# Gated norm of a hybrid gMLP/Mamba-2 layer: sums of squares by ones in column tiles, factors through memory, two gate blocks kept on chip

## The chip, the cores and the metric

The kernel runs on one core of a Trainium2 chip. The time is the device time of one execution in microseconds (us); of the kernel before there are three runs, 1413.58, 1413.98 and 1417.91 us, with the median 1413.98 us. One more execution was profiled. PE is TensorE (matrix products, and transposes as products with an identity), PEld its weight loads, DVE VectorE, ACT ScalarE, POOL GpSimd, and SP the engine that only issues loads. ACT issues all stores besides its own work.

## What is computed

One layer of a model with sequence length 1024 and width 1024, in float32. Of the reference these parts matter:

```python
y_a = spatial_gating(gelu(gm_u), gelu(gm_v), ...) * silu(gm_z)
y_b = ssd_scan(xh, dt, a, bm, cm) + xh * d_skip[:, None]          # 8 groups of 4 heads of 64 channels, chunks of 128
yz = (y_b.reshape(b, s, 2048) * silu(ssm_z)).reshape(b, s, 8, 256)
y_b = rms_norm(yz, ssm_norm_w.reshape(8, -1)).reshape(b, s, 2048)  # the gated norm: over 256 channels of a group
merged = sigmoid(g_a) * (y_a @ w_proj_a) + sigmoid(g_b) * (y_b @ w_proj_b)
x = x + gate[:, None, :] * (merged @ w_out)
return rms_norm(x, final_norm_w)
```

The gated norm needs for each group and each of the 1024 positions one factor, (sum of 256 squares / 256 + 1e-6) to the power -0.5.

## The kernel before

Channels lie on the 128 partitions and positions along the free dimension. Up to about 955 us the kernel makes the modulation, h and the large product with `w_in`. Then, to about 1150 us, it runs the SSD stage, to about 1319 us the second projection (units of p1, p2, p5, p3, p6, p7, p4), and last the product with `w_out`.

**The SSD stage** is a loop over 32 steps (L1434 on). A step is one group g of the eight and one s of 0 to 3, a quarter of the positions (256); the groups are taken in pairs, so the steps run 0_0, 1_0, 0_1, 1_1, 0_2 and so on, then 2_0, 3_0 on. A step takes some 6.3 us. In step n the program writes, in this order: `decay_rows` of step n+3 (ACT: two exponentials `ea`; POOL: an `AFFINE_SELECT` that masks `dcy`), `front` of step n (PE: `yi`, `sp`; DVE: `y1` and the state `st`; POOL: decay of the state), a few products of the first projection as filler (`proj_a`, tile `pma`, handed out by `draw`), `back` of step n (PE: `yn`; DVE: `ym`; POOL: `y` and then `yz`, the gated output), `prep_products` of step n+2 (PE: `pc`, `px`; DVE: `dcy` times `pc`), `decay_exps` of step n+3 (ACT: eight exponentials on `dcy`), `prep_b` of step n+2 (ACT: a copy `bn` of a part of `pc`, after which the PSUM bank of `pc` is given to the next tile that asks for one) and `fetch` of step n+6 (SP: loads of `dcy` and `sl`). From the last pair of products with `w_in` on, so in all that is told here, every engine runs its instructions in the order in which the program writes them.

**The factors before.** Two steps of a group fill one tile `yz` of 512 positions (q = 0 or 1). When it is full, `post` puts off the rest by slots of a task list (`later(k, f)`: f is written k slots on; a step has three slots): the stores of `yz` to `yb_d` after 3, the squares (ACT, and a sum of two halves on POOL) after 9, `post2` after 17. `post2` makes the column sums with `yz` as weights and a column of ones as moving operand: four products, each in two passes since the data are float32, with one PSUM column of 128 positions each (`pq`, 128x4). A slot later `post2b` brings them to `ssq` on DVE; with q = 1 (for groups 6 and 7 with each q) POOL takes the power -0.5 (`roots`), and 8 slots on `post3` transposes the 128x8 (or 128x4) of `ssq` on PE (`pr`; in the second projection the four of groups 6 and 7 go to a bank of `yp`), copies the rows on DVE and stores them to `rs_d`. The second projection loads `rs_d` as `rb` and `yb_d` as `yn`, multiplies them on DVE and splits the result on ACT (`p1bh`, with `p1a` for its weights).

**The first projection** `proj_a` (L1350) makes eight blocks dd of 128 rows in two halves: loads a gate `tha` on SP when the block begins, sums `pma`, multiplies (L1374) and stores to `mt_d` on ACT; the second projection loads that as `ma` (L1577) and adds it.

**Queues.** Stores stand in ACT's order among its arithmetic, loads in SP's order; an instruction that waits holds up those behind it on its engine. Each DMA also waits for an earlier one, some eight issues back, whose completion counter it takes over.

Of the kernel before, what the change touches and what calls it, by code (L numbers as in the profile page):

```python
# [35 lines left out]
def hybrid_kernel(  # L36
# [34 lines left out]
    rs_d = [dt_([1, S], f"rs_d{g}") for g in range(NG)]  # L71
    v_d = dt_([NG, P, NCH * P], "v_d")
# [887 lines left out]
    class Group:  # L960
# [158 lines left out]
        def post(self, q):  # L1119
# [8 lines left out]
            if g < NG - 2 or q == 0:  # L1128
                later(3, leave)
                later(9, self.squares, yz, [yz[:, j] for j in range(2)])  # L1130
                later(17, self.post2, q, yz[:, 0])
            else:
                wait = 1 if g < NG - 1 else 3
                later(wait, leave)
                sq = [turn(r, f"sq{g}", F32) for r in ((y1_r, ym_r) if g < NG - 1 else (war_r[0], war_r[0]))]
                later(wait, self.squares, yz, sq, pin)
                later(9, self.post2, q, sq[0])
# [6 lines left out]
        def post2(self, q, sq):  # L1144
            g = self.g
            pq = bank(f"pq{g}_{q}")
            for i in range(4):
                mm(pq[:, i : i + 1], sq[:, i * P : (i + 1) * P], ones[:, 0:1])
            later(1, self.post2b, q, pq)

        def post2b(self, q, pq):
            g = self.g
            V.tensor_scalar(ssq[:, g * NCH + q * 4 : g * NCH + q * 4 + 4], pq[:, 0:4], 1.0 / 256, EPS,
                            op0=ALU.mult, op1=ALU.add)
            release(f"pq{g}_{q}")
            if g >= NG - 2:
                self.roots(4 * q, 4)
            elif q == 1:
                self.roots(0, NCH)
                later(8, self.post3, 0, NCH)  # L1160

        def roots(self, c0, n):
            cs = slice(self.g * NCH + c0, self.g * NCH + c0 + n)
            G.tensor_tensor(ssq[:, cs], ssq[:, cs], nhalf[:, 0:n], op=ALU.pow)

        def post3(self, c0, n, at_once=False):

            g = self.g
            pr = rows_bank[0](f"pr{g}")
            tp(pr[0:n, 0:P], ssq[:, g * NCH + c0 : g * NCH + c0 + n], ident)  # L1170
            row = (cwt, tri)[g % 2][0:n, :]
            V.tensor_copy(row, pr[0:n, 0:P])
            release(f"pr{g}")
            to = rs_d[g].rearrange("o (c p) -> (o c) p", p=P)[c0 : c0 + n]
            if at_once:
                store(to, row)
            else:
                later(1, store, to, row)

    groups = [Group(g) for g in range(NG)]  # L1180
    rows_bank = [bank]
# [167 lines left out]

    def proj_a():  # L1350

        for dd in range(KT):
            if dd + 2 < KT:
                wa_load(dd + 2)
            ths, pms = [], []
            for h in range(2):
                th = turn(tha_r, f"tha{dd}_{h}", F32)
                load(th, th_d[dd * P : (dd + 1) * P, h * 512 : (h + 1) * 512])
                ths.append(th)
                pms.append(bank(f"pma{dd}_{h}"))  # L1360
            for k in range(KT):
# [9 lines left out]
                if k == 3 and 0 < dd < KT - 1:  # L1371
                    wa_low(dd + 1)
            for h in range(2):
                V.scalar_tensor_tensor(ths[h], ths[h], 1.0, pms[h], op0=ALU.add, op1=ALU.mult)  # L1374
                release(f"pma{dd}_{h}")
            for h in range(2):
                to = mt_d[dd][:, h * 512 : (h + 1) * 512]
                if dd < KT - 1:
                    later(1, store, to, ths[h])
                else:  # L1380
                    store(to, ths[h])
# [6 lines left out]
    fetch(3)  # L1388
    wa_load(1)
# [183 lines left out]
    def gate_load(b, h):  # L1573
        hs = slice(h * 512, (h + 1) * 512)
        th, ma = gate_slot(f"tg{b}_{h}"), gate_slot(f"ma{b}_{h}")
        load(th, th_d[(KT + b) * P : (KT + b + 1) * P, hs])
        load(ma, mt_d[b][:, hs])  # L1577
# [19 lines left out]
    def merged(b, h, c, name):  # L1597
# [3 lines left out]
        V.tensor_add(th, th, ma)  # L1601
        hi, lo = m_slot(f"mh{b}_{h}"), m_slot(f"ml{b}_{h}")
# [38 lines left out]
    for tags in (war_r[0][0][:2], wah_r[0][0][2:], wal_r[0][0][2:], y1_r[0], ym_r[0], tha_r[0]):  # L1641
# [20 lines left out]

    psx = psy = None
# [22 lines left out]
    for u, (nm, k) in enumerate(units):  # L1686
        if k == 0:
            if nm == "p1":
                psy = banks("yp2", "y")
                psx = banks("x", "x")  # L1690
                rows_bank[0] = lambda name: psy[int(name[2:]) - 6]
# [6 lines left out]
        if nm == "p1" and k % 4 < 2:  # L1698
# [141 lines left out]
```

## Time and profile before

| | |
|---|---|
| median of three runs | 1413.98 us (1413.58 to 1417.91) |
| the profiled execution, its own time | 1416.1 us |
| its span, first to last instruction | 1414.4 us |
| mean granted TensorE clock | 0.997 |
| DMA packets, bytes | 260524, 277.08 MB |
| loads (q1) and stores (q10), share of 16 DMA engines | 43.7%, 16.4% |
| POOL busy from 960 to 1140 us, in stretches of 20 us | 11.35 to 19.01 |

Views used: busy time of each engine in stretches of time; the waits of an engine by what ended them (total, times, longest); groups of instructions by tile; and the timeline of one engine (start, duration, engine, line, operation, output and inputs, count; in brackets the idle time before and what ended it). ACTq and SPq rows are DMA issues, whose duration is the issue, not the transfer. Times in the timeline are counted from the start of the span. Matmuls overlap, so what a group of them costs is read from start to start of the next group.

### The profile page before, as it was taken

To read this page: it belongs to the slowest core of one execution; us is meant where nothing else is said; L and a number is where in the kernel's file an instruction comes from. 1 tells how busy PE (TensorE), PEld (TensorE's weight loads), DVE (VectorE), ACT (ScalarE), POOL (GpSimd) and SP (SyncE) were. 2 spreads that over 40 slices of the span, in tenths; PEclk is the share of its full clock that TensorE was granted. 3 is DMA by queue.
4 is the path that set the end of the run, shared out by engine and by line. 5 is a ranking of instruction groups with operands and counts; after the bars stand their busy time and mean duration, and the time that the engine had idled before them with its cause. 6 is when DMAs were issued, how large, how long until landed. Compare 5 with 4: busy or idle time off the path is not lost.

```text
span 1414.4 us, 20499 instructions
## 1 busy us (share of the span) xinstructions
PE 1388.5 (98%) x7089; PEld 1151.3 (81%) x7089; DVE 1033.7 (73%) x1829; ACT 780.9 (55%) x1438; POOL 205.2 (15%) x192
## 2 busy tenths in 40 slices
PE   8999999999999999999999999999999999999997
PEld 7688888888888888888887888878888877888886
DVE  5686677776677888788888786567778767687743
ACT  6664575666566666555566555567667724233401
POOL 0000000000000000000010010027879760000000
PEclk9999999999999999999999999999999999999999
DMA  8552333333323677577676874598788758977432
GB/s 278 154 164 88 121 107 109 98 119 105 110 78 119 197 234 217 166 247 227 207 221 196 248 212 134 179 346 284 271 297 284 269 185 292 392 243 276 169 119 75
DMA packets 260524, 277.08 MB, mean 196 GB/s; under 512 B 13596, under 2 KB 210628, under 8 KB 260420
## 3 DMA queue, kind: packets, MB, share of 16 engines
q1 hardware_dynamic: 179396, 195.37, 43.7%
q10 hardware_dynamic: 81024, 80.40, 16.4%
q8 instruction: 56, 0.92, 0.3%
q14 instruction: 48, 0.39, 0.1%
HBM read 191.40 MB, written 84.31 MB: 195 GB/s over the span
## 4 chain that ended last, share of the span: by engine, by line
PE 82%; DMA 6%; DVE 4%; ACT 2%; issue 2%; POOL 1%; SPq 1%; ACTq 0%; POOLq 0%; DVEq 0%
PE xuz L585 6%; PE xcb L585 6%; PE po L90 6%; PE xx L585 6%; PE x L1568 5%; PE xz L585 5%; PE yp L1568 5%; PE xg L585 4%; PE pma L90 4%; PE yuz L585 3%; PE xv L585 3%; PE ycb L585 3%; PE yx L585 3%; PE yz L585 3%; PE yg L585 2%
## 5 line engine op out<-in xcount | busy, mean ns | idle before, releaser
L796 POOL TENSOR_TENSOR wog<-wog,gb 128x1024 f32<-128x1024 f32 x8 | 22.6, 2827 | 726.0 <-DMA wbr<-in_w_proj_b_dram 612.6
L56 ACT ACTIVATE dcy<-dcy,nacs 128x128 f32<-128x128 f32 x256 | 78.4, 389 | 33.7 <-POOL dcy L56 14.5
L56 POOL TENSOR_SCALAR_AFFINE_SELECT dcy<-dcy 128x1024 f32<-128x1024 f32 x32 | 36.4, 1137 | 109.5 <-ACT ea L56 109.4
L908 ACT ACTIVATE ac<-ac 128x1024 f32<-128x1024 f32 x32 | 34.0, 1062 | 20.6 <-DVE ac L906 20.4
L90 PE MATMUL pma<-yh,wah 128*128 128x512 f32 x128 | 43.1, 418 | 0.0
L90 PE MATMUL pma<-yh,wal 128*128 128x512 f32 x128 | 42.8, 415 | 0.0
L56 DVE TENSOR_TENSOR ym<-yn,ea 128x512 f32<-128x512 f32 (+1 forms) x32 | 19.9, 623 | 30.2 <-PE yn L90 30.0
L56 POOL TENSOR_TENSOR yz<-y,sl 128x512 f32<-128x512 f32 x32 | 41.2, 1286 | 0.6
L56 ACT ACTIVATE ea<-dcy 64x512 f32<-64x512 f32 x64 | 40.3, 629 | 1.5 <-DMA dcy<-acs_d 1.1
L56 DVE TENSOR_TENSOR dcy<-dcy,pc 128x1024 f32<-128x1024 f32 x32 | 39.0, 1218 | 2.9 <-PE pc L93 1.0
L90 PE MATMUL pma<-yl,wah 128*128 128x512 f32 x128 | 40.0, 393 | 0.0
L56 POOL TENSOR_TENSOR y<-y,ym 128x512 f32<-128x512 f32 (+1 forms) x32 | 36.6, 1143 | 17.2 <-DVE ym L56 16.5
L906 DVE SCALAR_TENSOR_TENSOR ac<-c2x,cwt,ac 128x1023 f32<-128x1023 f32 (+2 forms) x24 | 31.8, 1325 | 9.0 <-ACT ac L904 7.1
L1793 POOL TENSOR_TENSOR r<-r,fnw 128x256 f32<-128x256 f32 (+1 forms) x3 | 2.8, 918 | 238.3 <-ACT xr L1792 238.3
L1803 ACT ACTIVATE xr<-r 128x1024 f32<-128x1024 f32 x7 | 7.4, 1061 | 51.5 <-issue 39.0
L906 DVE SCALAR_TENSOR_TENSOR ac<-c2cb,cwt,ac 128x1023 f32<-128x1023 f32 (+2 forms) x24 | 30.6, 1276 | 7.1 <-ACT ac L904 5.7
L90 PE MATMUL yi<-dcy,xd 128*64 128x128 f32 x512 | 35.0, 279 | 0.6 <-DVE xe L56 0.6
L90 PE MATMUL sp<-xe,bn 128*128 128x256 f32 x112 | 32.7, 409 | 0.0
L90 PEld LDWEIGHTS yi<-dcy,xd 128*64 128x64 f32 x512 | 27.3, 136 | 4.8 <-issue 2.3
L906 DVE SCALAR_TENSOR_TENSOR ac<-c1cb,cwt,ac 128x1023 f32<-128x1023 f32 (+2 forms) x24 | 30.7, 1279 | 0.7 <-ACT ac L904 0.7
L906 DVE SCALAR_TENSOR_TENSOR ac<-c1x,cwt,ac 128x1023 f32<-128x1023 f32 (+2 forms) x24 | 30.7, 1278 | 0.0
L56 DVE SCALAR_TENSOR_TENSOR y<-sl,dskt,yi 128x256 f32<-128x256 f32 x64 | 27.7, 473 | 4.0 <-POOL yz L56 2.8
(2842 smaller groups left out, 4377.0 us busy)
## 6 DMA issues: line engine op xcount, KB each, us to landing
sl<-s_d SPq DMA_DIRECT2D x32, 768.0 KB
s_d<-ac ACTq DMA_DIRECT2D x32, 512.0 KB
dcy<-acs_d SPq DMA_DIRECT2D x32, 512.0 KB
aw<-in_ada_w_dram SPq DMA_DIRECT2D x16, 512.0 KB
wbr<-in_w_proj_b_dram SPq DMA_DIRECT2D x64, 128.0 KB
wb_d<-wbb ACTq DMA_DIRECT2D x32, 256.0 KB
wb_d<-wbc ACTq DMA_DIRECT2D x32, 256.0 KB
yb_d<-yz ACTq DMA_DIRECT2D x32, 256.0 KB
```

What stands on the lines that cost most here:

```text
L56: return lambda *a, **k: tc.keep_in_program_order(f(*a, **k))
L90: pin(PE.matmul(acc, l, r, start=first, stop=last))
L585: pin(PE.matmul(ps, lw[:, k * P : (k + 1) * P], r[k], start=first and n + k == 0, stop=n == 2 and k == 3, skip_group_check=not first))
L796: G.tensor_mul(w, w, gb)
L906: V.scalar_tensor_tensor(ac[:, s:], cc[:, : S - s], conv_wt[:, 3 - s, i : i + 1], ac[:, s:], op0=ALU.mult, op1=ALU.add)
L908: A.activation(ac, ac, AF.Silu)
L1568: pin(PE.matmul(ps[j], a[:, v, js], r, start=first and n + k == 0, stop=n == 2 and k == KT - 1, skip_group_check=not first))
L1793: G.tensor_mul(r[:, cs], r[:, cs], fnw[:, cs])
L1803: A.activation(xr, r, AF.Square, accum_out=sq[:, 0:1])
```

## The change

It has four parts.

1. `post2`: the weights are now 32 columns of ones and the squares move, 128 columns at a time, into four tiles of 32 PSUM partitions: `pq` is 128x128, each of its four strips holding 32 equal rows with the sums of 128 positions. DVE scales all 128x128 into one of three row tiles (`cwt`, `tri`, `par` in turn).
2. In place of power, transpose, copy and store: one row of each strip is stored to a new `ss_d` (4x128), five slots later loaded to `ssq` as 128x4, two slots later raised to the power on POOL, and one slot later stored to `rs_d` as 128x4. This is done for each g and q, so there are 16 powers of 128x4 (before: six of 128x8 and four of 128x4), 16 stores and 16 loads of `ss_d`, 16 stores of `rs_d` (before 10), and no transposes.
3. For q = 0 of groups 6 and 7 squares and `post2` come at slots 5 and 9 instead of 9 and 17; for their q = 1 the load, power and store are tied to units 2, 3 / 5, 6 / 7, 8 of the second projection.
4. `proj_a` loads a gate block one block ahead, and blocks 6 and 7 stay in their four slots of on-chip memory until `merged` has added them, so four stores to `mt_d` and four loads `ma` go; these four slots come back to the pool later, and one load of `wo` moves later.

```diff
...
     acs_d = dt_([NG, 4, HPG, 256], "acs_d")
     rs_d = [dt_([1, S], f"rs_d{g}") for g in range(NG)]
+    ss_d = [[dt_([1, 512], f"ss_d{g}_{q}") for q in range(2)] for g in range(NG)]
     v_d = dt_([NG, P, NCH * P], "v_d")
     ya_d = [dt_([P, S], f"ya_d{g}") for g in range(NG)]
...
                     store(yb_d[2 * g + j][:, q * 512 : (q + 1) * 512], yz[:, j])
             if g < NG - 2 or q == 0:
+                soon = 0 if g < NG - 2 else 4
                 later(3, leave)
-                later(9, self.squares, yz, [yz[:, j] for j in range(2)])
-                later(17, self.post2, q, yz[:, 0])
+                later(9 - soon, self.squares, yz, [yz[:, j] for j in range(2)])
+                later(17 - 2 * soon, self.post2, q, yz[:, 0])
             else:
                 wait = 1 if g < NG - 1 else 3
...
             keep(G.tensor_add(sq[0], sq[0], sq[1]))
         def post2(self, q, sq):
+            pq = bank(f"pq{self.g}_{q}")
+            for i in range(4):
+                mm(pq[32 * i : 32 * i + 32, 0:P], ones[:, 0:32], sq[:, i * P : (i + 1) * P])
+            later(1, self.post2b, q, pq)
+        def post2b(self, q, pq):
             g = self.g
-            pq = bank(f"pq{g}_{q}")
-            for i in range(4):
-                mm(pq[:, i : i + 1], sq[:, i * P : (i + 1) * P], ones[:, 0:1])
-            later(1, self.post2b, q, pq)
-
-        def post2b(self, q, pq):
-            g = self.g
-            V.tensor_scalar(ssq[:, g * NCH + q * 4 : g * NCH + q * 4 + 4], pq[:, 0:4], 1.0 / 256, EPS,
-                            op0=ALU.mult, op1=ALU.add)
+            n_row[0] += 1
+            row = (cwt, tri, par)[n_row[0] % 3]
+            V.tensor_scalar(row, pq[:, 0:P], 1.0 / 256, EPS, op0=ALU.mult, op1=ALU.add)
             release(f"pq{g}_{q}")
-            if g >= NG - 2:
-                self.roots(4 * q, 4)
-            elif q == 1:
-                self.roots(0, NCH)
-                later(8, self.post3, 0, NCH)
-
-        def roots(self, c0, n):
-            cs = slice(self.g * NCH + c0, self.g * NCH + c0 + n)
-            G.tensor_tensor(ssq[:, cs], ssq[:, cs], nhalf[:, 0:n], op=ALU.pow)
-
-        def post3(self, c0, n, at_once=False):
-
-            g = self.g
-            pr = rows_bank[0](f"pr{g}")
-            tp(pr[0:n, 0:P], ssq[:, g * NCH + c0 : g * NCH + c0 + n], ident)
-            row = (cwt, tri)[g % 2][0:n, :]
-            V.tensor_copy(row, pr[0:n, 0:P])
-            release(f"pr{g}")
-            to = rs_d[g].rearrange("o (c p) -> (o c) p", p=P)[c0 : c0 + n]
-            if at_once:
-                store(to, row)
-            else:
-                later(1, store, to, row)
+            later(1, store, ss_d[g][q].rearrange("o (i t) -> (o i) t", i=4),
+                  row.rearrange("(i r) t -> i r t", r=32)[:, 0])
+            if g < NG - 2 or q == 0:
+                later(5, self.sums_load, q)
+                later(7, self.roots, q)
+                later(8, self.rows_leave, q)
+        def part(self, q):
+            c0 = self.g * NCH + q * 4
+            return ssq[:, c0 : c0 + 4]
+        def sums_load(self, q):
+            load(self.part(q), ss_d[self.g][q].rearrange("o (p c) -> (o p) c", c=4))
+        def roots(self, q):
+            G.tensor_tensor(self.part(q), self.part(q), nhalf[:, 0:4], op=ALU.pow)
+        def rows_leave(self, q):
+            store(rs_d[self.g][:, q * 512 : (q + 1) * 512].rearrange("o (p c) -> (o p) c", c=4), self.part(q))
     groups = [Group(g) for g in range(NG)]
-    rows_bank = [bank]
+    n_row = [0]
     order = [(2 * r + j, s) for r in range(NG // 2) for s in range(4) for j in range(2)]
     done_f, done_d = [0], [0]
...
     p2qpool = tc.tile_pool(name="p2q", bufs=1, side="right", reuse_waits="tile")
     p2q = p2qpool.__enter__()
+    tha, kept = {}, {}
+    def tha_load(dd):
+        tha[dd] = []
+        for h in range(2):
+            th = turn(tha_r, f"tha{dd}_{h}", F32)
+            load(th, th_d[dd * P : (dd + 1) * P, h * 512 : (h + 1) * 512])
+            tha[dd].append(th)
     def proj_a():
         for dd in range(KT):
             if dd + 2 < KT:
                 wa_load(dd + 2)
-            ths, pms = [], []
-            for h in range(2):
-                th = turn(tha_r, f"tha{dd}_{h}", F32)
-                load(th, th_d[dd * P : (dd + 1) * P, h * 512 : (h + 1) * 512])
-                ths.append(th)
-                pms.append(bank(f"pma{dd}_{h}"))
+            ths, pms = tha.pop(dd), [bank(f"pma{dd}_{h}") for h in range(2)]
             for k in range(KT):
                 wh, wl = was[dd][k // 4]
...
                 if k == 3 and 0 < dd < KT - 1:
                     wa_low(dd + 1)
+                if k == 5 and dd < KT - 1:
+                    tha_load(dd + 1)
             for h in range(2):
                 V.scalar_tensor_tensor(ths[h], ths[h], 1.0, pms[h], op0=ALU.add, op1=ALU.mult)
                 release(f"pma{dd}_{h}")
             for h in range(2):
-                to = mt_d[dd][:, h * 512 : (h + 1) * 512]
-                if dd < KT - 1:
-                    later(1, store, to, ths[h])
+                if dd < KT - 2:
+                    later(1, store, mt_d[dd][:, h * 512 : (h + 1) * 512], ths[h])
                 else:
-                    store(to, ths[h])
+                    kept[dd, h] = ths[h], tha_r[0][(2 * dd + h) % 4]
     for r in (war_r, wah_r, wal_r):
         r[0][0].extend(room.pop(0) for _ in range(2))
...
     st_home = take("st_home", st_tag, F32)
     fetch(3)
+    tha_load(0)
     wa_load(1)
     fetch(5)
...
     def gate_load(b, h):
         hs = slice(h * 512, (h + 1) * 512)
-        th, ma = gate_slot(f"tg{b}_{h}"), gate_slot(f"ma{b}_{h}")
+        th = gate_slot(f"tg{b}_{h}")
+        ma = kept[b, h][0] if (b, h) in kept else gate_slot(f"ma{b}_{h}")
         load(th, th_d[(KT + b) * P : (KT + b + 1) * P, hs])
-        load(ma, mt_d[b][:, hs])
+        if (b, h) not in kept:
+            load(ma, mt_d[b][:, hs])
         gates[b, h] = th, ma
     mhl = {}
...
         V.scalar_tensor_tensor(th, th, 1.0, c, op0=ALU.add, op1=ALU.mult)
         V.tensor_add(th, th, ma)
+        if (b, h) in kept:
+            room.append(kept[b, h][1])
         hi, lo = m_slot(f"mh{b}_{h}"), m_slot(f"ml{b}_{h}")
         if name:
...
     draw(left[0] + 1)
     ya_free()
-    for tags in (war_r[0][0][:2], wah_r[0][0][2:], wal_r[0][0][2:], y1_r[0], ym_r[0], tha_r[0]):
+    for tags in (war_r[0][0][:2], wah_r[0][0][2:], wal_r[0][0][2:], y1_r[0], ym_r[0]):
         room.extend(tags)
     ps2.__exit__(None, None, None)
...
             V.tensor_sub(lo, f32(lo), f32(hi))
         wo[k] = wor.pop(k)
+    at_unit = {}
+    for i, g in enumerate(groups[NG - 2:]):
+        at_unit[2 + i] = [g.sums_load]
+        at_unit[5 + i] = [g.roots]
+        at_unit[7 + i] = [g.rows_leave]
     psx = psy = None
     sums, more = [], []
...
                 psy = banks("yp2", "y")
                 psx = banks("x", "x")
-                rows_bank[0] = lambda name: psy[int(name[2:]) - 6]
             elif nm == "p5":
                 psy = banks(f"y{nm}", "y")
...
             ps = psy if nm in ("p2", "p5", "p3") else psx
         multiply(u, ps)
-        if nm == "p1" and k % 4 < 2:
-            groups[NG - 2 + k % 4].post3(k // 4 * 4, 4, True)
+        for f in at_unit.get(u, ()):
+            f(1)
         due = more.pop(0) if k % 2 and more and u > 23 else None
         if k == KT - 1 and nm != "p4":
...
         if nm in ("p7", "p4") and k % 2 == 0:
             n = k // 2 + (4 if nm == "p4" else 0)
-            kept = 2 * (16 - len(mhl)) - len(places) - 3 * len(m_sl)
-            if len(room) >= 4 + kept and len(wor) + len(wo) < KT:
+            due_m = 2 * (16 - len(mhl)) - len(places) - 3 * len(m_sl)
+            if len(room) >= 4 + due_m and len(wor) + len(wo) < KT:
                 wo_load(KO[len(wor) + len(wo)])
         if nm == "p4" and k % 2 and wor:
```

The order shows where this stands. A row is line, operation, output<-inputs and shape; the number behind a name is that of a buffer, and the one before it the s of a step (`dcy_2`), or the q (`ss_d_1`). **ACT, steps 2_0 to 3_1 of the SSD stage**, before:

```order
L56 ACTIVATE yz_2_9078<-yz_2_9078 128x512 x2
L56 ACTIVATE dcy_2_9353<-dcy_2_9353,nacs 128x128 x8
L56 COPY bn_1_9511<-pc_1_9491 128x256
L56 ACTIVATE ea_2_9438<-dcy_2_9434 64x512 x2
L56 ACTIVATE yz_2_9168<-yz_2_9168 128x512 x2
L56 ACTIVATE dcy_2_9434<-dcy_2_9434,nacs 128x128 x8
L56 COPY bn_2_9585<-pc_2_9565 128x256
L56 ACTIVATE ea_3_9517<-dcy_3_9513 64x512 x2
L56 DMA yb_d_87<-yz_0_9399 128x512
L56 DMA yb_d_88<-yz_0_9399 128x512
L56 DMA mt_d_77<-tha_0_9151 128x512
```

and in the changed kernel, the same place:

```order
L56 ACTIVATE yz_2_9098<-yz_2_9098 128x512 x2
L56 DMA ss_d_0_68<-par 4x128
L56 ACTIVATE dcy_2_9369<-dcy_2_9369,nacs 128x128 x8
L56 COPY bn_1_9534<-pc_1_9513 128x256
L56 ACTIVATE ea_2_9455<-dcy_2_9451 64x512 x2
L56 ACTIVATE yz_2_9184<-yz_2_9184 128x512 x2
L56 DMA rs_d_58<-ssq 128x4
L56 ACTIVATE dcy_2_9451<-dcy_2_9451,nacs 128x128 x8
L56 COPY bn_2_9611<-pc_2_9589 128x256
L56 ACTIVATE ea_3_9540<-dcy_3_9536 64x512 x2
L56 DMA yb_d_103<-yz_0_9415 128x512
L56 DMA yb_d_104<-yz_0_9415 128x512
```

The store of the sums of the group at hand (`ss_d_0_68<-par`) now stands before the eight exponentials of one step, and the store of the factors of group 0 (`rs_d_58<-ssq`) before the eight exponentials `dcy_2_9451` and the copy `bn_2_9611` of the next.

**POOL, the same steps**, before:

```order
L56 TENSOR_TENSOR yz_2_9168<-yz_2_9168 128x512
L56 TENSOR_TENSOR y_1_9535<-y_1_9535,ym_1_9558 128x512
L56 TENSOR_TENSOR st_home<-st_home,cd 128x256
L56 TENSOR_TENSOR yz_0_9399<-y_1_9535,sl_1_9203 128x2x256
L56 AFFINE_SELECT dcy_3_9513<-dcy_3_9513 128x1024
L56 TENSOR_TENSOR st_1_1_9613<-st_0_2_9487,cd 128x256
L56 TENSOR_TENSOR y_1_9609<-y_1_9609,ym_1_9646 128x512
L56 TENSOR_TENSOR st_1_2_9650<-st_1_1_9613,cd 128x256
L56 TENSOR_TENSOR yz_0_9482<-y_1_9609,sl_1_9273 128x2x256
L56 AFFINE_SELECT dcy_3_9587<-dcy_3_9587 128x1024
```

and in the changed kernel:

```order
L56 TENSOR_TENSOR yz_2_9184<-yz_2_9184 128x512
L56 TENSOR_TENSOR y_1_9558<-y_1_9558,ym_1_9581 128x512
L56 TENSOR_TENSOR st_home<-st_home,cd 128x256
L56 TENSOR_TENSOR yz_0_9415<-y_1_9558,sl_1_9219 128x2x256
L56 TENSOR_TENSOR ssq<-ssq,nhalf 128x4
L56 AFFINE_SELECT dcy_3_9536<-dcy_3_9536 128x1024
L56 TENSOR_TENSOR st_1_1_9639<-st_0_2_9508,cd 128x256
L56 TENSOR_TENSOR y_1_9635<-y_1_9635,ym_1_9668 128x512
L56 TENSOR_TENSOR st_1_2_9672<-st_1_1_9639,cd 128x256
L56 TENSOR_TENSOR yz_0_9503<-y_1_9635,sl_1_9289 128x2x256
L56 TENSOR_TENSOR ssq<-ssq,nhalf 128x4
L56 AFFINE_SELECT dcy_3_9613<-dcy_3_9613 128x1024
```

The power (`ssq<-ssq,nhalf`), which the store above needs, stands behind the `yz` of the step, and ahead of the mask of a later `dcy`.

**ACT at the turn to the second projection**, before:

```order
L56 COPY p1bh_11306<-yn_0_11244 128x512
L56 COPY p1a_11246<-p1r_11247 128x512
L56 COPY p1bh_11338<-yn_0_11251 128x512
L56 COPY p1a_11253<-p1r_11254 128x512
L56 COPY p1bh_11374<-yn_0_11313 128x512
L56 COPY p1a_11315<-p1r_11316 128x512
L56 DMA mt_d_82<-tha_0_11260 128x512
L56 DMA mt_d_82<-tha_1_11263 128x512
L56 DMA rs_d_64<-cwt 4x128
L56 COPY p1bh_11450<-yn_0_11324 128x512
L56 COPY p1a_11326<-p1r_11327 128x512
L56 DMA rs_d_65<-tri 4x128
```

and in the changed kernel:

```order
L56 DMA rs_d_62<-ssq 128x4
L56 DMA ss_d_0_80<-par 4x128
L56 COPY p1bh_11325<-yn_0_11294 128x512
L56 COPY p1a_11296<-p1r_11297 128x512
L56 DMA rs_d_63<-ssq 128x4
L56 DMA yb_d_113<-yz_2_11174 128x512
L56 DMA yb_d_114<-yz_2_11174 128x512
L56 ACTIVATE sq_11289<-yz_2_11174 128x512
L56 ACTIVATE sq_11290<-yz_2_11174 128x512
L56 DMA rs_d_64<-ssq 128x4
L56 COPY p1bh_11349<-yn_0_11299 128x512
L56 COPY p1a_11301<-p1r_11302 128x512
```

The stores of `tha` to `mt_d` are gone, and stores of factors and sums have come between the copies `p1bh` and `p1a`.

## The prediction

> **What bounds the kernel now.** I read the busy shares first, then the busy time in stretches of the SSD stage, the waits of PE, and the timelines of POOL, ACT and PE side by side.
>
> ```profile
> PE 1388.5 (98%) x7089; PEld 1151.3 (81%) x7089; DVE 1033.7 (73%) x1829; ACT 780.9 (55%) x1438; POOL 205.2 (15%) x192
> 1040.00:1060.00 20.00, 18.84 (x150) 16.44 (x148) 12.10 (x24) 10.19 (x28) 11.35 (x12) 1.00 0.97 333
> 1060.00:1080.00 20.00, 18.48 (x142) 16.36 (x142) 17.92 (x29) 15.43 (x45) 18.64 (x20) 1.00 0.69 236
> 1160.00:1180.00 20.00, 17.05 (x75) 13.07 (x74) 9.85 (x20) 4.46 (x8) 2.99 (x3) 1.00 0.87 294
> PE pc L90 <- DVE tha L56: 2.6, 1, 2.6
> PE px L93 <- ACT bn L56: 1.2, 1, 1.2
> ```
>
> The first row is the whole span; the next three give in 20 us the busy time of PE, PEld, DVE, ACT and POOL, then the clock, the DMA share and GB/s; the last two are waits of PE in all. PE sets the time: 1388.5 of 1414.4 us busy, and a microsecond taken from or added to its chain is one of the result. But the 15% of POOL mislead: in the SSD stage it is busy up to 18.64 of 20 us, and ACT 15.43 besides its stores. That PE waits for `bn` (a PSUM bank that ACT must empty) at all, and for so little, says that the three engines run a loop with little slack there. So I price the change twice: what PE's own work saves, and what it adds to that loop.
>
> **Savings on PE.** The sums and transposes, and the nearest row for the new form:
>
> ```profile
> 1043.56 0.95 PE L90 MATMUL pq<-ones,yz 128*128 128x1 f32 x8
> 1044.37 0.27 PE L93 MATMUL pr<-ident,ssq 128*8 128x128 f32 x1
> 1044.57 1.09 PE L90 MATMUL yi<-dcy,xd 128*64 128x128 f32 x16
> 1045.60 1.13 PE L90 MATMUL sp<-xe,bn 128*128 128x256 f32 x4
> 37.93 1.07 PE L90 MATMUL pm<-aw,scz 128*32 128x256 f32 x16
> 38.93 0.66 PE L93 MATMUL px<-ident,x 128*128 128x128 f32 x4
> ```
>
> From start to start a `pq` takes 0.81 us and a `pr` 0.20. The new `pq` is eight passes with 32 columns of weights and 128 moving columns. `pm` has the same weights with 256 moving columns: 16 in 1.00 us, so at most 0.50 for eight; if it goes by columns, half, 0.25. `yi`, 64 wide with 128 columns, is 16 in 1.03, again 64 ns each, so I stay near the upper end: 0.46, a saving of 0.35 (bounds 0.31 and 0.56). Sixteen give 5.6 us (5.0 to 9.0); five of them fall where PE is going to wait anyway (below), so 11 x 0.35 = 3.9. Ten transposes at 0.20 (the four of `yp` taken as `pr`): 2.0. Sum 5.9.
>
> On the column tiles the Trainium skill, TensorEngine Tiling (Array Packing), section Tiling Modes (Key Properties), speaks against this: a change of the tiling mode drains the array, twice for each `pq`. With a drain at the 0.27 us that a single product takes above, the two would eat the whole 0.35, and the saving would be 2.0 instead of 5.9; `yi` changes to 64-wide tiles and back in each step, and its 64 ns hold such costs already, so I do not add one.
>
> DVE loses ten copies and has 128x128 where it had 128x4. No row has that shape; it lies between the 128x4 and a 128x512 product from PSUM:
>
> ```profile
> L56 DVE TENSOR_SCALAR ssq<-pq x16: 140/152/158, 995.5 to 1166.2; 128x4 f32<-128x4 f32 x16
> L56 DVE TENSOR_TENSOR ym<-yn,ea 128x512 f32<-128x512 f32 (+1 forms) x32 | 19.9, 623 | 30.2 <-PE yn L90 30.0
> ```
>
> By columns that is 0.15 + (0.62 - 0.15) / 4 = 0.27, so 0.12 more sixteen times, against ten copies of 128 columns that go: nothing, on an engine with 27% to spare.
>
> **The two blocks kept and the turn.** Four stores and four loads go, and the turn, from 1160 to 1180 us, is where PE was idle 2.95 of 20 us. There ACT stood idle so long before `p1bh`:
>
> ```profile
> 1174.90 0.28 ACTq L56 DMA_DIRECT2D rs_d<-cwt  x1
> 1175.28 0.62 ACT L56 CAST p1bh<-yn 128x512 fp32r<-128x512 f32 x1 [12.30 <-PE x L1568]
> ```
>
> The store of `rs_d`, and the stores of `tha` ahead of it in ACT's order, held up `p1bh`, which PE needs. At best the 2.9 go, at worst none or as much comes on top, since new stores of sums and factors stand between the copies `p1bh` now: I take 1.5. The loads of `tha` go out a block of some 25 us earlier in SP's order, which can only ease the 2.6 us above; that is counted with the stall below.
>
> **The new chain in the SSD stage.** What the change moves into ACT's and POOL's order weighs more. Take steps 2_1 and 3_1, POOL, then ACT, then PE:
>
> ```profile
> 1011.64 1.29 POOL L56 TENSOR_TENSOR y<-y,ym 128x512 f32<-128x512 f32 x1 [0.79 <-DVE ym L56]
> 1012.87 0.62 POOL L56 TENSOR_TENSOR st_home<-st_home,cd 128x256 f32<-128x256 f32 x1
> 1013.45 1.31 POOL L56 TENSOR_TENSOR yz<-y,sl 128x512 f32<-128x512 f32 x1
> 1014.70 1.10 POOL L56 TENSOR_SCALAR_AFFINE_SELECT dcy<-dcy 128x1024 f32<-128x1024 f32 x1
> 1163.16 1.01 POOL L56 TENSOR_TENSOR ssq<-ssq,nhalf 128x4 f32<-128x4 f32 x1 [5.24 <-DVE ssq L56]
> 1009.07 2.45 ACT L56 ACTIVATE dcy<-dcy,nacs 128x128 f32<-128x128 f32 x8
> 1013.07 0.37 ACT L56 COPY bn<-pc 128x256 f32<-128x256 f32 x1 [1.55 <-DVE dcy L56]
> 1013.34 1.27 ACT L56 ACTIVATE ea<-dcy 64x512 f32<-64x512 f32 x2
> 1042.98 0.36 ACTq L56 DMA_DIRECT2D rs_d<-cwt  x1
> 1016.15 1.05 PE L90 MATMUL yn<-sl,st 128*128 128x128 f32 x8
> ```
>
> Before, the eight exponentials began at 1009.07, `bn` was copied by 1013.44, and `yn`, which takes the bank that it empties, began at 1016.15: 2.7 us of slack. Now the store of group 0's factors stands before the exponentials, it needs POOL's power, and this stands behind `yz`, done at 1014.76. So: power 1.01, issue 0.36, exponentials 2.45, `bn` 0.37, together 4.19 behind the end of `yz`, is 1018.95, and `yn` is 2.8 us late. The load of the sums is written three slots before and hides in a step; if it does not, the wait is longer. The same sum at the four other places, first the end of `yz`, then the piece of PE that takes the bank:
>
> ```profile
> 1040.73 1.29 POOL L56 TENSOR_TENSOR yz<-y,sl 128x512 f32<-128x512 f32 x1
> 1069.08 1.27 POOL L56 TENSOR_TENSOR yz<-y,sl 128x512 f32<-128x512 f32 x1
> 1094.26 1.29 POOL L56 TENSOR_TENSOR yz<-y,sl 128x512 f32<-128x512 f32 x1
> 1118.92 1.30 POOL L56 TENSOR_TENSOR yz<-y,sl 128x512 f32<-128x512 f32 x1
> 1042.46 0.39 PE L90 MATMUL pc<-sl 128*128 128x128 f32 x2
> 1070.42 0.39 PE L90 MATMUL pc<-sl 128*128 128x128 f32 x2
> 1096.50 0.39 PE L90 MATMUL pc<-sl 128*128 128x128 f32 x2
> 1121.00 0.60 PE L90 MATMUL yn<-sl,st_home 128*128 128x128 f32 x4
> ```
>
> 1042.02 + 4.19 - 1042.46 = 3.8; 1070.35 gives 4.1; 1095.55, 3.2; 1120.22, 3.4. With the first, 17.3 us.
>
> In each pair the factors of the other group follow one step on, now in a closed loop: from `bn` two `ea` 1.27, mask 1.10, `y` 1.29, `yz` 1.31 and again 4.19, so 9.2 us, and 10.4 with two decays of the state (0.62), before the next bank is free. PE came to that bank so much after the first; the shortest and the longest of the five are
>
> ```profile
> 1047.02 0.63 PE L90 MATMUL pma<-yh,wah 128*128 128x512 f32 x2
> 1128.95 0.38 PE L93 MATMUL px<-ident,sl 128*128 128x128 f32 x2
> ```
>
> the second of the two at 1047.02, about 1047.25, 4.8 us after 1042.46, and 1128.95, 7.95 after 1121.00. Late by 9.2 - 4.8 = 4.4 and, with 1.1 for squares that ACT has in between there, 10.4 + 1.1 - 7.95 = 3.5; the other three, 6.7 to 7.9 apart, by about 2.4 each: in all 15.
>
> Less what is counted double: the long powers of 1.65 us, which sat ahead of `yz` in two of these places, move away (-3.4), and a stall that was there before is overlapped:
>
> ```profile
> 1023.01 1.65 POOL L56 TENSOR_TENSOR ssq<-ssq,nhalf 128x8 f32<-128x8 f32 x1
> 1054.46 1.86 ACT L56 ACTIVATE dcy<-dcy,nacs 128x128 f32<-128x128 f32 x6 [7.18 <-DMA yb_d<-yz]
> ```
>
> ACT stood 7.18 us before these exponentials, and PE lost 2.6 for `tha` and some tenths behind it: -3. Loss: 17.3 + 15 - 3.4 - 3 = 26.
>
> **Sum.** 26 - 5.9 - 1.5 = +18.6 us on the profiled 1416.1, 1434.7; the median of the runs lies 2.1 lower, so 1432.6, say 1432.
>
> **Rivals.**
>
> Only the first of each pair costs. If PE, once late, gives ACT and POOL the time to run ahead, the second event falls within the delay of the first. For it: `bn` had 2.7 us of slack. Against: the loop above goes through PE's own `yn`, which is late too. 17.3 - 6.4 - 7.4 = +3.5, 1417 (1412 to 1424).
>
> Hidden. The power could be written so early, or POOL have so much room, that ACT never waits; then only the savings count: -7.4 to -12, 1402 to 1407. For it: 15% of POOL. Against: the order of both engines, and 18.64 of 20.
>
> Transfers add to the chain. A store that waits for a counter of a load ahead of it (as in the 7.18 us above) now stands at ten more places, and the small loads sit in SP's order between transfers at a DMA share of 0.69 to 0.97. With 1 to 3 us at each of ten: +29 to +49, 1442 to 1462.
>
> The clock. In the trace PE ends at 1406.5, and
>
> ```profile
> 1406.00:1410.00 4.00, 0.67 (x6) 0.47 (x4) 2.47 (x10) 0.51 (x2) 0.73 (x1) 1.00 0.00 0
> 1410.00:1414.00 4.00, 0.00 (x0) 0.00 (x0) 0.73 (x3) 0.72 (x1) 0.00 (x0) 0.52 0.34 131
> ```
>
> some 3.5 us of idleness brought the granted clock to 0.52. Three of my stalls are as long (3.8, 4.1, 4.3). If each cost half of a following step of 6.3 us, 3 x 3 = 9 more: 1441. The rule is in the Trainium skill, TensorE: Matmul & The Clock Gate, Part 1: after an idle window of about 3.4 us the gate passes half the pulses; the windows run free, so a gap barely longer rarely holds a whole one, and the trace's end agrees in size.
>
> **How the numbers follow.** The forecast 0.55 (1423 to 1441), only the first 0.17, hidden 0.11, transfers 0.13, clock 0.04. The range 1408 to 1448 leaves out hidden and the far half of the transfers. A measurement of this kernel can tell some 0.3%, 4 us. Faster: hidden 0.11 and 0.02 of the second case; same: 0.06 of the second; slower: the rest, 0.81.
>
> **What would show it.** In the changed kernel's profile ACT's exponentials behind `rs_d<-ssq` start some 1.4 us after the end of a `yz`, with idle time of 3 to 7 us before them put down to POOL `ssq`; PE waits of 2 to 4 us for `bn`, or what hangs on it, come in ten places between 1010 and 1140 us, and the stretches there show PE at 15 to 18 of 20; before 990 us nothing changes. The `pq` groups take 0.25 to 0.50 us, `pr` and `ma` of blocks 6 and 7 are gone, and the turn loses up to 3 us of idleness. I am wrong if PE stays at 19 to 20 there, above all if `yz` comes earlier than I let it, or if ACT waits for DMA and not for POOL.

## The result

The changed kernel takes 1445.7 us (median of 6 runs, 1444.7 to 1449.7), the kernel before beside it 1415.37 (6 runs): a ratio of 1.0218, 95% interval 1.0202 to 1.0233, so some 31 us slower. The forecast was 1432 with a range to 1448; way, place and mechanism were right, and the loss larger. (The ratios are not those of the two medians and can differ a little from them.)

The page's busy row and the busy time in stretches of 20 us (PE, PEld, DVE, ACT, POOL, clock, DMA share, GB/s) of the changed kernel:

```profile
span 1444.0 us, 20504 instructions
PE 1393.8 (97%) x7079; PEld 1147.2 (79%) x7079; DVE 1033.6 (72%) x1819; ACT 778.3 (54%) x1438; POOL 207.4 (14%) x198
980.00:1000.00 20.00, 19.65 (x159) 16.50 (x158) 16.55 (x30) 15.61 (x40) 14.64 (x14) 1.00 0.92 324
1000.00:1020.00 20.00, 16.92 (x122) 13.88 (x122) 12.26 (x22) 9.38 (x25) 14.86 (x17) 0.91 0.81 271
1040.00:1060.00 20.00, 12.85 (x91) 10.23 (x90) 9.19 (x17) 8.48 (x25) 10.92 (x10) 0.93 0.86 279
1140.00:1160.00 20.00, 14.83 (x112) 12.22 (x111) 8.83 (x17) 10.26 (x27) 11.46 (x13) 0.91 0.41 120
1200.00:1220.00 20.00, 20.00 (x90) 16.57 (x89) 14.23 (x23) 9.93 (x18) 2.49 (x2) 1.00 0.90 264
```

Up to 1000 us nothing is lost, and from 1200 us PE is full again; in between it is busy 12.85 to 18.9 of each 20 us. PE is idle 50.2 us in all (before 25.9). It is also busy 5.3 us longer with less work: the granted clock, 1.00 all through these stretches before, is down to 0.83 to 0.93 in six of the ten from 1000 to 1200 us. The waits (total, times, longest) name the releaser, those of PE first, then one of ACT:

```profile
PE pc L91 <- ACT bn L56: 7.9, 3, 2.7
PE px L94 <- ACT bn L56: 6.0, 4, 3.1
PE yn L91 <- ACT bn L56: 5.8, 2, 3.3
PE pma L91 <- ACT bn L56: 4.5, 1, 4.5
PE pq L91 <- POOL sq L56: 4.5, 1, 4.5
ACT dcy L56 <- POOL ssq L56: 47.8, 8, 7.1
```

PE waits for `bn` 24.2 us in ten pieces, where it had waited 1.2 in one, and ACT waits, ahead of its exponentials, for POOL's power. The first event, steps 2_1 and 3_1, in the timelines of POOL, ACT and PE:

```profile
1010.17 1.30 POOL L56 TENSOR_TENSOR yz<-y,sl 128x512 f32<-128x512 f32 x1
1011.41 1.03 POOL L56 TENSOR_TENSOR ssq<-ssq,nhalf 128x4 f32<-128x4 f32 x1
1012.85 0.69 ACT L56 ACTIVATE dcy<-dcy,nacs 128x128 f32<-128x128 f32 x2 [7.06 <-POOL ssq L56]
1015.20 0.35 ACT L56 COPY bn<-pc 128x256 f32<-128x256 f32 x1
1015.60 1.57 PE L91 MATMUL yn<-sl,st 128*128 128x128 f32 x8 [2.53 <-ACT bn L56]
```

The exponentials start 1.38 us behind the end of `yz` (1.37 was forecast), `bn` ends 4.08 behind it (4.19), and `yn` waits 2.5 us (2.8). The chain of waits between 1000 and 1140 us, shares by line, shows how the bound moved; before, then the changed kernel:

```profile
by line: PE pma L90 23.7%; PE yi L90 12.7%; PE sp L90 12.4%; PE yn L90 9.7%; PE pc L90 5.4%; PE px L93 5.1%; PE pq L90 5.1%; POOL yz L56 3.4%; issue 2.6%; PE pc L93 2.6%; POOL dcy L56 2.3%; DVE wal L56 2.2%; ACT dcy L56 1.7%; ACT ea L56 1.7
by line: issue 13.2%; ACT dcy L56 11.6%; POOL yz L56 10.0%; POOL dcy L56 8.1%; POOL y L56 7.8%; POOL ssq L56 6.4%; ACT ea L56 5.8%; PE pma L91 5.0%; DMA yb_d<-yz 5.0%; ACTq L56 4.0%; DMA dcy<-acs_d 3.1%; DMA sl<-s_d 3.0%; PE yn L91 2.4%; PE
```

Before, most pieces are PE's; after, the loop that was forecast, from ACT's exponentials over POOL's mask, `y`, `yz` and power back to ACT, makes up the largest part of the chain.

### The profile page after: what moved, and what is told of

Its sections match the earlier page's. It is cut to its first block, busy times and chain, and to the rows that moved or that the text cites. A ratio compares the mean times of both kernels' runs of the same rounds, so it can differ in the third digit from the quotient of the medians.

```text
span 1444.0 us, 20504 instructions
## 1 busy us (share of the span) xinstructions
PE 1393.8 (97%) x7079; PEld 1147.2 (79%) x7079; DVE 1033.6 (72%) x1819; ACT 778.3 (54%) x1438; POOL 207.4 (14%) x198
## 4 chain that ended last, share of the span: by engine, by line
PE 80%; POOL 5%; ACT 4%; DVE 3%; DMA 3%; issue 3%; SPq 1%; ACTq 1%; POOLq 0%; DVEq 0%
PE xx L586 6%; PE x L1574 6%; PE xuz L586 6%; PE po L91 6%; PE xcb L586 6%; PE xz L586 5%; PE xg L586 5%; PE yp L1574 5%; PE yuz L586 3%; PE yx L586 3%; PE xv L586 3%; PE ycb L586 3%; PE pma L91 3%; PE yz L586 2%; PE yg L586 2%
## 5 line engine op out<-in xcount | busy, mean ns | idle before, releaser
L91 PE MATMUL pc<-sl 128*128 128x128 f32 x128 | 27.0, 295 | 7.9 <-ACT bn L56 7.9
L91 PEld LDWEIGHTS pma<-yh,wah 128*128 128x128 f32 x128 | 24.4, 193 | 10.6 <-ACT bn L56 5.4
L94 PE MATMUL px<-ident,sl 128*128 128x128 f32 x128 | 26.4, 291 | 6.0 <-ACT bn L56 6.0
```

What stands on the lines that cost most here:

```text
L91: pin(PE.matmul(acc, l, r, start=first, stop=last))
L94: pin(PE.transpose(dst, src, idn))
```

## The experiments

The kernels were measured in four groups, and those of a group share their runs of the kernel before (medians 1416.42, 1416.74, 1416.98 and 1417.09 us). Differences between groups are read from the ratios.

| kernel | us | ratio to before, 95% interval |
|---|---|---|
| wait_alone | 1454.31 | 1.0269 (1.0252 to 1.0286) |
| store_later | 1416.21 | 0.9998 (0.9985 to 1.0011) |
| power_earlier | 1421.39 | 1.0037 (1.0023 to 1.0050) |
| odd_store_later | 1427.27 | 1.0064 (1.0048 to 1.0081) |
| blocks_only | 1408.51 | 0.9942 (0.9928 to 0.9957) |
| squares_later | 1411.88 | 0.9962 (0.9950 to 0.9974) |
| blocks_leave_later | 1411.96 | 0.9967 (0.9956 to 0.9979) |
| both_later | 1408.70 | 0.9938 (0.9925 to 0.9951) |
| spare_products | 1447.76 | 1.0210 (1.0191 to 1.0228) |
| sums_twice_together | 1407.17 | 0.9925 (0.9909 to 0.9940) |
| sums_twice_apart | 1409.70 | 0.9940 (0.9925 to 0.9956) |
| half_the_sums | 1405.62 | 0.9919 (0.9906 to 0.9933) |

### The wait alone, in the kernel before

```diff
             release(f"pq{g}_{q}")
+            if g < NG - 2 or q == 0:
+                later(7, self.spare_power)       # POOL: par[:, 0:4] <- ones ** nhalf
+                later(8, self.spare_store, q)    # ACT: par[:, 0:4] to spare memory
             if g >= NG - 2:
```

> The kernel before with ten-plus-two spare powers of 128x4 on POOL and as many spare stores of 128x4 on ACT, at the slots where the changed kernel has its powers and stores of factors; no small loads, no new form of the sums, no kept blocks; the computation is otherwise whole. Theory of the wait: it is the loss by itself; waits of PE for bn of 20 us and more, a granted clock near 0.989, and 1435 to 1455 us. Rival, transfers (the loads and the stores of sums) or products: 1414 to 1422 us.

Measured 1454.3, +38 us: more than the whole change costs, with fourteen spare powers and stores and without one small load, one new product or one kept block. The same place in its timelines of POOL and ACT, and ACT's wait:

```profile
1015.60 1.03 POOL L56 TENSOR_TENSOR par<-ones,nhalf 128x4 f32<-128x4 f32 x1
1017.03 0.69 ACT L56 ACTIVATE dcy<-dcy,nacs 128x128 f32<-128x128 f32 x2 [7.06 <-POOL par L56]
ACT dcy L56 <- POOL par L56: 58.1, 9, 7.7
```

A power and a store of 2 KB that nobody needs hold ACT 7.06 us, as long as the real ones do. So the wait suffices. The 38 us are not its price in the changed kernel, though: here the six long powers of 1.65 us stay beside the spare ones, and in the changed kernel they are gone. That the powers as such, 1 us each on POOL, are not the loss, store_later shows next: it has sixteen of them.

### The store behind the exponentials; the power ahead of yz

```diff
-                later(8, self.rows_leave, q)
+                later(9, self.rows_leave, q)
```

> The changed kernel with the store of the factors one slot later, so that in ACT's order it stands behind the eight exponentials, the copy bn and the two ea of the next step; all transfers, powers and products stay. Theory of the wait (ACT held before the exponentials by POOL's power is the loss, and the lowered clock follows from it): the waits of PE for bn, 24 us in the changed kernel, fall under 3, the granted clock is back at 0.997, and the time is 1404 to 1412 us, that is under the kernel before, as the new sums and the missing transposes then count. Rival, transfers (sixteen small loads and sixteen more stores take turns and counters from the others): stays at 1432 to 1446. Rival, products (the new form of the sums and its 128x128 on VectorE): stays above 1425.

```diff
-                later(7, self.roots, q)
+                later(6, self.roots, q)
```

> The changed kernel with POOL's power one slot earlier, so ahead of y and yz of its step; the store of the factors stays where it is, before the exponentials, and all transfers stay. Theory of the wait: the store finds its power done, so ACT's idle time put down to POOL ssq, 47.8 us in the changed kernel, falls under 10, and the time is 1405 to 1418 us; the power then delays y by up to 1 us in ten places. Rival, the store as such (its issue or the counter that it waits for holds ACT before the exponentials, whatever POOL does): 1430 to 1446. Rival, transfers: 1432 to 1446.

One slot for the store takes 2.2% off, from 1.0218 to 0.9998; one slot for the power, with the store left in place, 1.8%. Neither transfers nor products nor the store as such can be the bulk of the loss. The 2.2%, some 31 us, are what the wait costs in the changed kernel. Between the two traces, 28.3 us apart, PE's idle time falls by 19.1 us (50.2 to 31.1) and its busy time, with the same products, by 9.2 (1393.8 to 1384.6), while the clock rises from 0.989 to 0.995. But store_later stays at 1416, not at the 1404 to 1412 expected: PE still waits 8 us for `bn` (under 3 expected), 6.4 of them behind two ACT stalls:

```profile
1053.20 2.44 ACT L56 ACTIVATE dcy<-dcy,nacs 128x128 f32<-128x128 f32 x8 [7.68 <-DVE ym L56]
1126.96 1.15 ACT L56 ACTIVATE yz<-yz 128x512 f32<-128x512 f32 x2 [7.99 <-DMA yb_d<-yz]
```

power_earlier misses its 1405 to 1418 as well, at 1421: ACT still waits 22.6 us in all for the power (under 10 expected), which now stands behind `st` and the sum of squares.

### Does each event of a pair cost?

```diff
-                later(8, self.rows_leave, q)
+                later(8 + g % 2, self.rows_leave, q)
```

> The changed kernel with the store of the factors one slot later for the odd groups only (the second of each pair); the even groups keep theirs before the exponentials. Theory of the loop (the two events of a pair cost one after the other, since the second runs through PE's own late yn): the second waits go, 13 to 15 us, and the first, 17, stay: 1428 to 1436 us. Rival, only the first of each pair costs: nothing changes, 1442 to 1448 us.

Measured 1427.3, a little under the range given for the loop: without the second events some 22 us of the loss go (ratio 1.0218 to 1.0064), where 13 to 15 were expected, and the five first ones still show, 14.4 us of waits for `bn` by `pc` and `yn`. The rival "only the first of each pair costs" falls.

### The kept blocks alone

The kernel before with the diff's `proj_a`, `tha_load`, `gate_load`, `merged` and what belongs to them:

```diff
+                if k == 5 and dd < KT - 1:
+                    tha_load(dd + 1)
...
+                    kept[dd, h] = ths[h], tha_r[0][(2 * dd + h) % 4]
```

> The kernel before with the fourth part alone: gate blocks loaded one block ahead, blocks 6 and 7 kept on chip. Theory of the wait: this part has no share in the loss; the stall at 940 to 960 us shrinks by 2 to 3 us and the turn by 1 to 3, so 1408 to 1414 us. Rival, blocks (the four slots that come back late and the loads moved ahead in SP's order delay others): 1420 us or more.

Measured 1408.5, -8 us: at the better end, and the first version that is faster than both kernels. Where it comes from, a row of PE before, then PE's share of the span and the turn in blocks_only:

```profile
948.62 0.49 PE L90 MATMUL pc<-sl 128*128 128x128 f32 x2 [2.64 <-DVE tha L56]
```

```profile
PE 1386.1 (99%) x7089; PEld 1150.4 (82%) x7089; DVE 1034.5 (74%) x1829; ACT 780.2 (55%) x1438; POOL 205.3 (15%) x192
1160.00:1180.00 20.00, 20.00 (x92) 16.23 (x90) 13.91 (x25) 9.08 (x17) 0.00 (x0) 1.00 0.85 296
```

The wait for `tha` at 948.6 us is gone (the load stood behind two of `wa` in SP's order), and the turn, idle 2.95 us before, is full. The wait had cost more than its 2.64 us: from 940 to 960 us PE was busy 17.36 of 20 us before at a granted clock of 0.91 (0.50 for some 3.4 us behind the wait), and in blocks_only 18.73 at 1.00. Over the span PE's idle time falls by 5.2 us and its busy time by 2.4. What the new sums bring is not read from +38 and -8, since wait_alone has more powers than the change; it is read from both_later below.

### Why do the new sums not pay? The two stalls

```diff
-                soon = 0 if g < NG - 2 else 4
+                soon = 0 if g < NG - 2 else 2
```

> The kernel with the store of the factors a slot later (store_later), and the squares and sums of q = 0 of groups 6 and 7 two slots later than in the change (7 and 13 in place of 5 and 9). In store_later ACT stood 8.0 us before these squares, put down to the store of yz, and PE then 3.4 us for bn. Theory, the squares overwrite yz and so wait until its store has landed, at the head of ACT's order: the PE wait goes, 1409 to 1413 us. Rival, counters (another store would hold ACT there in any case): within 2 us of store_later, 1414 to 1418.

```diff
-                    later(1, store, mt_d[dd][:, h * 512 : (h + 1) * 512], ths[h])
+                    later(3, store, mt_d[dd][:, h * 512 : (h + 1) * 512], ths[h])
```

> The store_later kernel with the stores of the gate blocks to mt_d two slots later, so that they stand behind the next eight exponentials, bn and ea in ACT's order. In store_later ACT stood 7.7 us at 1045 to 1053 behind the store of sums and the two stores of tha, which take over counters of loads of 256 and 768 KB, and PE 3.1 us for bn. Theory, counters (these stores wait for the landing of loads that go out late, and the extra small transfers have shifted which): the wait goes or moves behind the exponentials, 1409 to 1414 us. Rival, the small store of sums alone holds ACT: within 2 us of store_later, 1414 to 1418.

> Both of the two edits on store_later. If the two waits are what keeps the new sums from paying, PE is idle little more than with the kept blocks alone (20.7 us of 1406.8) and does some 8 us less work: 1398 to 1406 us, the fastest so far. If new waits take their place: 1407 to 1414.

All three stand on store_later, whose edit they keep. Each of the two alone takes some 0.3% off it, in the range that its theory gave. For the squares the traces agree: they overwrite `yz` and waited 7.99 us for its store to land, and in squares_later this wait is gone, with PE's 3.4 us behind it. For the stores of `tha` they don't: in the trace of blocks_leave_later, its slowest execution of twelve, ACT stands 6.82 us at the same place (7.68 in store_later), now with the small store of sums, and no store of `tha`, ahead, and PE still waits 2.2 us; so why this version is faster is not shown. Together they give 1408.7, not the 1398 to 1406 hoped for: PE is busy 1380.0 us, 6.1 less than in blocks_only, and the time is the same, so idle time has taken the place of the work. The chain of waits of both_later from 1000 to 1140 us, in its slowest execution of six:

```profile
by line: DMA dcy<-acs_d 23.7%; POOL yz L56 14.5%; issue 9.1%; POOL y L56 6.7%; POOL dcy L56 6.5%; ACT dcy L56 4.9%; ACTq L56 4.6%; DMA yb_d<-yz 4.2%; DMA sl<-s_d 3.0%; SPq L100 2.9%; PE pma L91 2.6%; DMA ssq<-ss_d 2.0%; POOL st_home L56 1.9
```

In blocks_only the first entry is `PE pma` with 18.6%, and most that follow are PE's; here they are loads of `dcy`, which SP issues among the small loads, and POOL. In sums_twice_together, below, which is this kernel with more work for PE, `PE pma` is first again with 16.3%, and the loads of `dcy` have 5.3%: the chains are about equally long, and none of them alone is shown to hold the time.

### Is TensorE's work worth its length there?

Two kernels on both_later, with each set of products issued twice. The second set right behind the first:

```diff
-            for i in range(4):
-                mm(pq[32 * i : 32 * i + 32, 0:P], ones[:, 0:32], sq[:, i * P : (i + 1) * P])
+            for _ in range(2):
+                for i in range(4):
+                    mm(pq[32 * i : 32 * i + 32, 0:P], ones[:, 0:32], sq[:, i * P : (i + 1) * P])
```

> The both_later kernel with the four products of each sum issued twice, the second set right behind the first (they write the same result). This is the price of the products without any change of the array's tiling: 16 x 0.36 = 5.8 us, so 1413 to 1416 us.

The second set in `post2b`, a slot later, instead:

> The both_later kernel with the four products of each sum issued twice, the second set a slot later, apart from the first. Theory of the drain (each way into and out of the 32-column tiles stops TensorE for some 0.2 us, seen as idleness put down to issue before pq and yi): 16 x (0.36 + 0.4) = 12 us, so 1419 to 1423 us, some 6 above sums_twice_together. Rival, no drain (the 0.81 us of the old form fell by the whole 0.45): the same as sums_twice_together within 2 us.

On blocks_only, with the old form of the sums, half of them left out (the other half stands in for them):

```diff
-            for i in range(4):
+            for i in range(2):
                 mm(pq[:, i : i + 1], sq[:, i * P : (i + 1) * P], ones[:, 0:1])
```

> The blocks_only kernel (the kernel before with the kept blocks, 1408.5 us) with two of the four products of each sum left out: the sums of half the positions are not computed, and those of the other half stand in for them. This takes 16 x 0.40 = 6.5 us of work from TensorE in the same tiling, with no transfer, store or power added. Theory of the forecast (in the SSD stage what is taken from TensorE's chain is one of the result): 1401 to 1403 us. Rival (the stage is so near the loop through POOL and ScalarE that TensorE then waits instead, as the doubled sums, which cost nothing, suggest): 1405 to 1409 us.

Doubled in one place the sums cost nothing (0.9925 against 0.9938, within the intervals), where 5.8 us were expected: with the new path of factors PE has that much slack. Apart they cost some 2 us more than that (0.9940, the intervals overlap), where 6 were expected for the drain. Idle time for a drain is there all the same, as the groups by tile show, `pq`'s idle time before it that is put down to issue, in both_later and in sums_twice_apart (total, times):

```profile
  issue: 1.9, 9
```

```profile
  issue: 7.8, 27
```

That is 0.2 to 0.3 us each time; sums_twice_together has the 1.9 us in 9 places too, so it goes with the entry and not with the products, and blocks_only, with the old form, has none. With the old path, half the sums left out give 0.9919 against 0.9942, 3 of 6.5 us, as the rival had it. In the traces PE's busy time falls by 6.3 us and its idle time grows by 3.0, so even there a microsecond less of PE's work is worth about a half. The size is uncertain, since by the two intervals it could be 0.4 to 6 us. The premise of the forecast, one for one, holds in neither test as it stood.

### The clock

```diff
         step(n, "back")
+        if n in (15, 19, 23, 24):
+            spare(5)          # ten more products into pma; before `back` for n in (11, 27)
```

> The changed kernel with ten spare products of 128x512 (some 2.3 us) on TensorE ahead of the instruction that waits, at six of its long waits for bn (2.5 to 3.3 us each); they repeat a product of the first projection, so y_a's projection is wrong in size, nothing else. Theory, the lowered clock costs time of its own (some 14 us of TensorE work at half clock in the changed kernel, of which the forecast counted nothing): TensorE is hardly idle at these places, the granted clock rises from 0.989 to 0.995 or more, and the time falls although 14 us of work are added: 1434 to 1441 us. Rival, the low clock is hidden in waits that POOL and ScalarE set: 1444 to 1448. Rival, the added work is not hidden: 1452 to 1460.

Measured 1447.8: 14 us of added work cost nothing that the runs can tell (ratio 1.0210 against 1.0218), as the first rival had it. So PE's idleness at these places is slack of the loop through ACT and POOL, and work there is hidden. The granted clock, though, stayed at 0.990 instead of the 0.995 expected: it fell at other waits, which had grown (`px` at 1027.0 us waits 2.3 us, in the changed kernel 0.7). So the run doesn't tell how much the low clock costs.

## Why the prediction was right, and where its sizes were off

**The chain.** Right as put: store before the exponentials, power behind `yz`, both events of a pair. The first waits were 2.5, 2.6, 2.7, 2.6 and 3.3 us (forecast 2.8, 3.8, 4.1, 3.2, 3.4), and of the second ones the longest was the one forecast with 4.4:

```profile
1056.91 0.61 PE L91 MATMUL pma<-yh,wah 128*128 128x512 f32 x1 [4.52 <-ACT bn L56]
```

The second waits were shorter than forecast, 10.5 us for 15. That the idleness, 24.2 us, is close to the 26 is chance: the waits forecast add up to 32, and the 26 are what two deductions left of them. And the term was too small: in the changed kernel the wait costs 31 us (store_later), more than PE idles for it. One deduction was misread. PE's wait of 2.6 us for `tha`, taken as lost behind ACT's stall at 1054.5 us, stands at 948.6 us, and behind the stall PE lost 1.2 (`px` at 1057.2); both are gone with the fourth part alone (blocks_only), so they were no saving of the chain. And the clock, put down as a rival with 0.04, came on top of the forecast case. The first event, busy time and clock in stretches of 2 us:

```profile
1012.00:1014.00 2.00, 1.07 (x5) 0.55 (x3) 1.27 (x3) 1.16 (x4) 0.45 (x1) 1.00 0.68 178
1014.00:1016.00 2.00, 0.40 (x3) 0.41 (x4) 0.00 (x0) 2.00 (x7) 0.00 (x0) 1.00 0.96 320
1016.00:1018.00 2.00, 2.00 (x12) 2.00 (x12) 0.69 (x1) 0.70 (x2) 1.20 (x2) 0.55 1.00 257
1018.00:1020.00 2.00, 2.00 (x19) 1.36 (x19) 1.45 (x2) 0.00 (x0) 2.00 (x3) 0.60 1.00 388
```

After 2.5 us of idleness PE's clock is 0.55 and 0.60 in the next two stretches (0.50 for some 3.4 us, cut finer), and `yn`, which is part of the loop, took 1.57 us in place of 1.05. PE's busy time, 1393.8, is 9.2 above that of store_later and 13.8 above that of both_later (1380.0), which has the same sums and the clock at 0.998. How much of this lengthens the run stays open.

The whole, step by step back from the change: the wait 31 us (store_later), the two edits against the stalls some 8 (both_later), the new sums nothing, and the kept blocks -8 (blocks_only); the forecast had 26, nothing outside its rival on transfers, -5.9 and -1.5. In another order the steps could come out otherwise.

**The sums.** The product term was right in what it priced: `pq` takes 0.36 us from start to start (0.25 to 0.50 forecast, 0.46 taken), DVE 0.28 for 128x128 (0.27). Of the forecast saving of 5.9, transposes included, nothing reached the time (0.9938 in both_later, 0.9942 in blocks_only), by two failed steps. "A microsecond taken from its chain is one of the result" does not hold in this stage: half the sums left out gave about a half, and doubled sums cost nothing. And the change of tiling, which I did not add because `yi` holds it already, is idle time of 0.2 us ahead of 9 of the 16 `pq` (both_later). The Trainium skill, TensorEngine Tiling (Array Packing), Tiling Modes, says that a change of the tiling mode drains TensorE. The trace agrees, as far as idle time put down to issue can show a drain; some 2 of the 6 us expected for it reached the time in sums_twice_apart.

**The kept blocks and the turn.** 1.5 us forecast, 8 measured alone. I had counted only the 2.9 us of the turn, by half, left the wait for `tha` to the overlapped stall, and not looked at the clock behind it. In the changed kernel the turn itself lost instead: before its sums of group 7, PE waits 4.5 us, since ACT's stores ahead of the squares wait 3.6 us for a small load (`ssq<-ss_d`).

```profile
1189.64 0.43 PE L91 MATMUL pq<-sq,ones 128*32 128x128 f32 x8 [4.51 <-POOL sq L56]
```

**The rivals.** Hidden and first-only are refuted (wait_alone, odd_store_later). Transfers adding to the chain were not what made the change slow, but waits behind transfers are part of what is left once the wait is gone (store_later at 1416, and its 7.99 us for the store of `yz`). The clock was given 0.04 and worked out for stalls of some 3.5 us and more, from the end of the trace; in the same trace it had fallen behind the 2.64 us at 948.6.

## What to carry to other kernels

Where engines run in program order, a store is a wait: before moving one, look at what it waits for and at what stands behind it on its engine, and put it behind the work that another engine needs next. Here one slot was worth 2.2%. A busy share of 98% for one engine does not make each of its microseconds count; the chain of waits in the stage does, and here taking work from the busiest engine paid about half or nothing, because another loop was nearly as long. Test the parts of a change apart: this one held a gain of 0.6% (blocks_only) under a loss of 2.2% (store_later).

## What the runs showed of the hardware

The clock can fall after less idleness than I had thought. In the changed kernel 2.53 us without a product (1013.07 to 1015.60) were enough for some 3.4 us at 0.50, and 2.74 us ahead of 1081.68 for some 6 us; in the kernel before it was the 2.64 us ahead of 948.62. But it need not: these two gaps of the changed kernel left the clock at 1.00.

```profile
1047.89 0.49 PE L91 MATMUL pc<-sl 128*128 128x128 f32 x2 [2.63 <-ACT bn L56]
1112.98 0.49 PE L91 MATMUL pc<-sl 128*128 128x128 f32 x2 [2.56 <-ACT bn L56]
```

What decides between them, no run here shows. The Trainium skill, TensorE: Matmul & The Clock Gate, Part 1, gives a window of about 3.4 us of idleness; a gap of 2.5 us holds no such window whole, so the measured rows go further than the rule. And entering 32-column tiles showed as some 0.2 us of idle time in 9 of 16 places (both_later), which the profile books to nothing but "issue".
